# Row-wise infinity norm of an 8192 x 8192 float32 matrix: another split of the rows over partitions, the last quarter of them in smaller pieces, and the result stored in three parts

## The chip, the cores and the metric

The kernel runs on one core of one Trainium2 chip. The time is device microseconds of one execution, and a lower time is better. The core has a vector engine (DVE in the profile), which does all the arithmetic here, a sync engine (SP) and a scalar engine (ACT) whose queues issue transfers, and 16 DMA engines that carry the transfers between HBM and the on-chip memory SBUF. SBUF has 128 partitions, and the vector engine works on all of them side by side, each with its own stretch of data.

## The reference

For every row of the matrix the largest absolute value is wanted.

```python
def setup_inputs():
    rows = 8192
    cols = 8192
    return {
        "x": np.random.randn(rows, cols).astype(np.float32),
    }

def reference(x):
    return np.linalg.norm(x, ord=np.inf, axis=1)
```

The input has 8192 x 8192 x 4 bytes = 268.4 MB, and each element is read once. The output has 8192 numbers, 32 KB.

## The kernel before

The 8192 rows are 64 for each of the 128 partitions, and the kernel takes them two at a time (B = 2), so that there are 32 tiles. One tile `t` holds, in each partition, two adjacent rows, which are 16384 elements or 64 KB; over all partitions it has 8.39 MB. Two loops run over the tiles: the outer one over A = 8 blocks of 1024 rows, the inner one over N = 4 tiles in a block. Within a block each partition owns 8 adjacent rows (4 tiles of 2), so the addresses that neighbouring partitions read at the same time lie 8 rows of 32 KB apart, which is 256 KB.

For each tile, line 70 issues one load on the queue of the sync engine, and line 71 reduces it on the vector engine: one instruction reads 128 x 2 x 8192 elements and writes two numbers in each partition, the largest absolute values of the two rows, into `r_all`. The branch with `split` is never taken, since `split` is False. After the loops, line 78 stores `r_all` in one transfer, whose pieces in HBM are 8 numbers (32 bytes) long.

The pool `sbuf` has three buffers for `t`. The order on each engine is the order of the program. A load can be issued once the buffer that it goes into has been read by the reduce of three tiles earlier; the queue therefore holds up to three loads. Each load and store also takes one of eight completion semaphores (DMAHW0 to DMAHW7) in turn, and a transfer that gets a semaphore again waits, on the engine that issues it, until the transfer that had it before has landed.

Of the kernel before, what the change touches and what calls it, by code (L numbers as in the profile page):

```python
# [1 line left out]
logging.getLogger("concourse").setLevel(logging.ERROR)  # L3

# [1 line left out]

# [4 lines left out]


@with_exitstack
def kernel(
    ctx: ExitStack,
    tc: tile.TileContext,
    x: bass.AP,
    out: bass.AP,
    A: int = 8,
    B: int = 2,  # L20
    K: int = 4,
    BUFS: int = 3,
):
    nc = tc.nc
    P = nc.NUM_PARTITIONS

    rows, cols = x.shape
    assert rows % P == 0
    n_tiles = rows // P

    assert n_tiles % (A * B) == 0
    N = n_tiles // (A * B)
    x_t = x.rearrange("(a p n b) c -> a n p (b c)", p=P, a=A, n=N, b=B)
    out_t = out.rearrange("(a p n b) -> p a n b", p=P, a=A, n=N, b=B)

    bc = cols * B
    c_k = bc // K

    sbuf = ctx.enter_context(tc.tile_pool(name="sbuf", bufs=BUFS))
    outp = ctx.enter_context(tc.tile_pool(name="outp", bufs=1))  # L40

    r_part = outp.tile([P, N, K], mybir.dt.float32)
    r_all = outp.tile([P, A, N, B], mybir.dt.float32)

    for a in range(A):
        split = False
        for n in range(N):
            t = sbuf.tile([P, bc], x.dtype)
            t_b = t.rearrange("p (b c) -> p b c", b=B, c=cols)
            src = x_t[a, n]  # L50
            if split:
                for k in range(K):
                    nc.sync.dma_start(
                        out=t[:, k * c_k : (k + 1) * c_k],
                        in_=src[:, k * c_k : (k + 1) * c_k],
                    )
                    nc.vector.reduce_max(
                        out=r_part[:, n, k : k + 1],
                        in_=t[:, k * c_k : (k + 1) * c_k],
                        axis=mybir.AxisListType.X,  # L60
                        apply_absolute_value=True,
                    )
                nc.vector.reduce_max(
                    out=r_all[:, a, n, :],
                    in_=t_b[:],
                    axis=mybir.AxisListType.X,
                    apply_absolute_value=True,
                )
            else:
                nc.sync.dma_start(out=t[:], in_=src)  # L70
                nc.vector.reduce_max(  # L71
                    out=r_all[:, a, n, :],
                    in_=t_b[:],
                    axis=mybir.AxisListType.X,
                    apply_absolute_value=True,
                )

    nc.sync.dma_start(out=out_t[:], in_=r_all[:])


# [1 line left out]
_INS = ['x']  # L82
_OUTS = [((8192,), 'float32')]


# [23 lines left out]
```

## Time and profile before

| | before |
|---|---|
| median of 10 runs | 644.94 us (644.73 to 645.41) |
| the profiled execution | 644.73 us, span 642.7 us from the first to the last instruction |
| vector engine busy | 551.0 us, 86% of the span, 32 instructions |
| loads | 32, in 4096 packets of 64 KB (one for each partition and tile) |
| result's store | 1, 32 KB in 1024 packets of 32 bytes |
| bytes read from HBM | 268.44 MB, 418 GB/s over the span |

The span runs from the first instruction to the last; the time has about 2 us more, which lie around it. In the views of the profile, "SPq" is the queue of the sync engine, and "A <- B" in a wait reads "A waited for B". "DMA share" is the mean busy share of the 16 DMA engines, so 1.00 means that all of them were moving data all the time. The count of packets on the page, 5648, is the 4096 packets of the loads, the 1024 of the store, and 16 short completion packets for each of the 33 transfers (528). The figures in GB/s by slices of the span jump between 392 and 457, a step of 65 GB/s: in a slice of 16.07 us that is one packet of 64 KB more or less on each of the 16 engines.

### The profile page before, as it was taken

The numbers are of one execution on the slowest core, as the hardware profiler recorded it, in microseconds if no ns is written. First come the engines' busy times: TensorE is split into PE (matmuls) and PEld (weight loads), VectorE is DVE, ScalarE is ACT, GpSimd is POOL, SyncE is SP. The second block draws the span as 40 slices with busy tenths as digits, with TensorE's granted clock in tenths as the row PEclk, the third lists the DMA queues.
The fourth block names the chain that finished last, engine by engine and source line by source line (L and its number), as shares of the span: only waits on it lengthen the run. The fifth ranks groups of instructions, "written<-read, shape, count | busy, mean of one in ns | idle before, by whom it ended". The sixth has DMA issues, their size and how long they took to land.

```text
span 642.7 us, 139 instructions
## 1 busy us (share of the span) xinstructions
DVE 551.0 (86%) x32; POOL 0.2 (0%) x4
## 2 busy tenths in 40 slices
DVE  0588898888998888998888998888988888988888
POOL 0000000000000000000000000000000000000000
DMA  9999999999999999999999999999999999999960
GB/s 392 457 412 436 457 392 457 441 408 457 441 408 457 436 412 457 424 424 457 392 457 453 396 457 441 408 457 436 412 457 420 428 457 392 457 453 396 457 261 2
DMA packets 5648, 268.47 MB, mean 418 GB/s; under 512 B 1552, under 2 KB 1552, under 8 KB 1552
## 3 DMA queue, kind: packets, MB, share of 16 engines
q1 hardware_dynamic: 5648, 268.47, 96.6%
HBM read 268.44 MB, written 0.03 MB: 418 GB/s over the span
## 4 chain that ended last, share of the span: by engine, by line
DMA 70%; DVE 29%; issue 0%; SPq 0%
DMA t<-in_x_dram 70%; DVE r_all L71 29%; SPq L70 0%
## 5 line engine op out<-in xcount | busy, mean ns | idle before, releaser
L71 DVE TENSOR_REDUCE r_all<-t 128x2 f32<-128x16384 f32 x32 | 551.0, 17220 | 88.7 <-DMA t<-in_x_dram 88.7
L93 POOL MEMSET const-bfloat16-1.0<- 128x1 bf16 x1 | 0.1, 101 | 0.0
L93 POOL MEMSET const-uint8-127<- 128x1 uint8 x1 | 0.1, 101 | 0.0
L93 POOL MEMSET const-float32-0.0<- 128x1 f32 x1 | 0.1, 98 | 0.2 <-issue 0.2
L93 POOL MEMSET const-float32-1.0<- 128x1 f32 x1 | 0.1, 98 | 0.0
## 6 DMA issues: line engine op xcount, KB each, us to landing
t<-in_x_dram SPq DMA_DIRECT2D x32, 40.8
out_dram<-r_all SPq DMA_DIRECT2D x1, 32.0 KB, 2.2
```

The source lines that it names most:

```text
L71: nc.vector.reduce_max(out=r_all[:, a, n, :], in_=t_b[:], axis=mybir.AxisListType.X, apply_absolute_value=True,)
L93: nc = _bacc.Bacc("TRN2", target_bir_lowering=False, num_devices=1)
```

## The change

The rows are cut into two parts.

- **The bulk** is the first three quarters, 6144 rows, 48 for each partition. It is read in 24 tiles of two rows, each by one load of 64 KB per partition and one reduce, as before. There is one block (A = 1) in place of eight, so that each partition owns 48 adjacent rows (G = 24 tiles of B = 2), and neighbouring partitions read at addresses 1.5 MB apart. The 48 results of a partition lie in `r_bulk`, and one store issued on the queue of the scalar engine writes them (line 73), in pieces of 192 bytes.
- **The tail** is the last quarter, 2048 rows, 16 for each partition, which lie 512 KB apart from partition to partition. It goes through the same three buffers, two rows to a tile, but each row is loaded and reduced on its own, in the pieces that the table `TAIL` gives: eight rows whole (8192 elements, 32 KB per partition), five in halves, two in quarters, and the last one in pieces of 2048, 2048, 2048, 1024, 512 and 512 elements (8 KB down to 2 KB per partition). That is 32 loads and 32 reduces, where there were 8 and 8.
- **The partial results** of the tail's first 15 rows go into `part`, four places to a row, cleared by a memset at the start; one small reduce over `part` gives these rows' results in `r_tail`, and the scalar engine's queue stores them (line 88). The last row's first five pieces leave their results in the tile itself, in the spare columns just behind the row, so that the reduce of the last piece reads 512 elements and these five together and writes the row's final result to `r_fin`. The sync engine's queue stores that (line 99): one number for each partition.

```diff
+TAIL = (
+    [[8192]] * 8
+    + [[4096, 4096]] * 5
+    + [[2048] * 4] * 2
+    + [[2048, 2048, 2048, 1024, 512, 512]]
+)
...
-    A: int = 8,
+    G: int = 24,
     B: int = 2,
-    K: int = 4,
     BUFS: int = 3,
...
-    x_t = x.rearrange("(a p n b) c -> a n p (b c)", p=P, a=A, n=N, b=B)
-    out_t = out.rearrange("(a p n b) -> p a n b", p=P, a=A, n=N, b=B)
...
+    n_tail = len(TAIL)
+    assert n_tail % B == 0
+    n_bulk_rows = rows // P - n_tail
+    assert n_bulk_rows % (G * B) == 0
+    A = n_bulk_rows // (G * B)
+    split = n_bulk_rows * P
+    x_b = x[:split].rearrange("(a p n b) c -> a n p (b c)", p=P, a=A, n=G, b=B)
+    out_b = out[:split].rearrange("(a p n b) -> p a (n b)", p=P, a=A, n=G, b=B)
+    x_t = x[split:].rearrange("(p t b) c -> t p (b c)", p=P, b=B)
+    out_t = out[split:].rearrange("(p t) -> p t", p=P)
...
+    part = outp.tile([P, n_tail - 1, k_max], F32)
+    nc.vector.memset(part[:], 0.0)
+
+    def absmax(o, i):
+        nc.vector.reduce_max(out=o, in_=i, axis=X, apply_absolute_value=True)
 
     for a in range(A):
...
+        for n in range(G):
+            t = sbuf.tile([P, B * cols + 16], F32, tag="t")
+            nc.sync.dma_start(out=t[:, : B * cols], in_=x_b[a, n])
+            absmax(
+                r_bulk[:, a, n * B : (n + 1) * B],
+                t[:, : B * cols].rearrange("p (b c) -> p b c", b=B),
+            )
+    nc.scalar.dma_start(out=out_b, in_=r_bulk[:])
+
+    for i in range(0, n_tail, B):
+        t = sbuf.tile([P, B * cols + 16], F32, tag="t")
+        for j in range(B):
+            r = i + j
+            at = j * cols
+            last = r == n_tail - 1
+            for k, w in enumerate(TAIL[r]):
+                nc.sync.dma_start(
+                    out=t[:, at : at + w], in_=x_t[i // B][:, at : at + w]
+                )
+                if last and k == k_last - 1:
+
+                    absmax(r_tail[:, : n_tail - 1], part[:])
+                    nc.scalar.dma_start(
+                        out=out_t[:, : n_tail - 1], in_=r_tail[:, : n_tail - 1]
                     )
...
+                    absmax(r_fin[:], t[:, at : B * cols + k_last - 1])
+                elif last:
+                    absmax(
+                        t[:, B * cols + k : B * cols + k + 1], t[:, at : at + w]
                     )
...
+                else:
+                    absmax(part[:, r, k : k + 1], t[:, at : at + w])
+                at += w
+    nc.sync.dma_start(out=out_t[:, n_tail - 1 :], in_=r_fin[:])
```

On the sync engine's queue the end of the program stood like this before: seven of the 32 loads of whole tiles, the last one `t_156`, then the store.

```order
L70 DMA t_138<-in_x_dram 128x16384 [waits DMAHW6_49,DVE_49]
L70 DMA t_141<-in_x_dram 128x16384 [waits DMAHW7_49,DVE_49]
L70 DMA t_144<-in_x_dram 128x16384 [waits DMAHW0_49,DVE_49]
L70 DMA t_147<-in_x_dram 128x16384 [waits DMAHW1_49,DVE_49]
L70 DMA t_150<-in_x_dram 128x16384 [waits DMAHW2_49,DVE_49]
L70 DMA t_153<-in_x_dram 128x16384 [waits DMAHW3_49,DVE_49]
L70 DMA t_156<-in_x_dram 128x16384 [waits DMAHW4_49,DVE_49]
L78 DMA out_0_dram<-r_all_62 128x8x8 [waits DVE_49]
```

On the same queue the end is now this; `t_190` is the last tile, with the tail's rows 14 and 15.

```order
L82 DMA t_190<-in_x_dram 128x2048 [waits DMAHW7_49,DVE_49]
L82 DMA t_190<-in_x_dram 128x2048 [waits DMAHW0_49]
L82 DMA t_190<-in_x_dram 128x2048 [waits DMAHW1_49]
L82 DMA t_190<-in_x_dram 128x2048 [waits DMAHW2_49]
L82 DMA t_190<-in_x_dram 128x2048 [waits DMAHW3_49]
L82 DMA t_190<-in_x_dram 128x2048 [waits DMAHW4_49]
L82 DMA t_190<-in_x_dram 128x2048 [waits DMAHW6_49]
L82 DMA t_190<-in_x_dram 128x1024 [waits DMAHW7_49]
L82 DMA t_190<-in_x_dram 128x512 [waits DMAHW0_49]
L82 DMA t_190<-in_x_dram 128x512 [waits DMAHW1_49]
L99 DMA out_0_dram<-r_fin_63 128x1 [waits DMAHW2_49,DVE_49]
```

The last tile's one load has become ten. Only the first of them waits for the buffer (DVE); every one waits for the landing of the transfer that had its semaphore before, eight transfers earlier. DMAHW5 is skipped here, since the store of `r_tail` on the scalar engine's queue takes it. The store at the end waits for the final reduce alone and for a landing long past.

On the vector engine the last instructions are now these; before, there was one reduce of 128 x 16384 elements for each tile and nothing else.

```order
L63 TENSOR_REDUCE part_64<-t_190 128x1 [waits DMAHW2_49]
L63 TENSOR_REDUCE r_tail_62<-part_64 128x15 [waits DVE_49]
L63 TENSOR_REDUCE t_190<-t_190 128x1 [waits DMAHW3_49]
L63 TENSOR_REDUCE t_190<-t_190 128x1 [waits DMAHW4_49]
L63 TENSOR_REDUCE t_190<-t_190 128x1 [waits DMAHW6_49]
L63 TENSOR_REDUCE t_190<-t_190 128x1 [waits DMAHW7_49]
L63 TENSOR_REDUCE t_190<-t_190 128x1 [waits DMAHW0_49]
L63 TENSOR_REDUCE r_fin_63<-t_190 128x1 [waits DMAHW1_49,DVE_49]
```

Each reduce now waits for its own piece. The reduce that fills `r_tail` stands ahead of the last row's six, though the source has it behind five of them, and its store can go out while the last row is still on its way.

More of the change, by code (lines that the diff above doesn't have):

```diff
@@ L10 @@
 from concourse._compat import with_exitstack
+F32 = mybir.dt.float32
+X = mybir.AxisListType.X
+TAIL = (
[4 more added lines that the diff above has]
+)
 @with_exitstack
@@ L27 @@
     rows, cols = x.shape
[L28 to L32, printed above, removed]
-    x_t = x.rearrange("(a p n b) c -> a n p (b c)", p=P, a=A, n=N, b=B)
-    out_t = out.rearrange("(a p n b) -> p a n b", p=P, a=A, n=N, b=B)
-    bc = cols * B
-    c_k = bc // K
+    n_tail = len(TAIL)
[4 more added lines that the diff above has]
+    split = n_bulk_rows * P
@@ L39 @@
+    x_b = x[:split].rearrange("(a p n b) c -> a n p (b c)", p=P, a=A, n=G, b=B)
+    out_b = out[:split].rearrange("(a p n b) -> p a (n b)", p=P, a=A, n=G, b=B)
+    x_t = x[split:].rearrange("(p t b) c -> t p (b c)", p=P, b=B)
+    out_t = out[split:].rearrange("(p t) -> p t", p=P)
     sbuf = ctx.enter_context(tc.tile_pool(name="sbuf", bufs=BUFS))
     outp = ctx.enter_context(tc.tile_pool(name="outp", bufs=1))
-    r_part = outp.tile([P, N, K], mybir.dt.float32)
-    r_all = outp.tile([P, A, N, B], mybir.dt.float32)
@@ L45 @@
-    for a in range(A):
[L46 to L55, printed above, removed]
-                    )
[L57 to L61, printed above, removed]
-                    )
[L63 to L76, printed above, removed]
@@ L78 @@
-    nc.sync.dma_start(out=out_t[:], in_=r_all[:])
+    k_last = len(TAIL[-1])
+    r_bulk = outp.tile([P, A, G * B], F32)
+    r_tail = outp.tile([P, n_tail], F32)
+    r_fin = outp.tile([P, 1], F32)
+    k_max = max(len(r) for r in TAIL[:-1])
+    part = outp.tile([P, n_tail - 1, k_max], F32)
+    nc.vector.memset(part[:], 0.0)
+    def absmax(o, i):
+        nc.vector.reduce_max(out=o, in_=i, axis=X, apply_absolute_value=True)
+    for a in range(A):
+        for n in range(G):
[5 more added lines that the diff above has]
+            )
```

## The prediction

> **What bounds the kernel now.** I read the chain of work that ended last, then the windows by stage, then the groups and the waits. The chain of the page says that transfers and reduces share the end of the program, and its pieces in order of time show how:
>
> ```profile
> DMA 70%; DVE 29%; issue 0%; SPq 0%
> ...
> 0.73 0.38 SPq L70
> 1.11 0.06 issue
> 1.17 40.73 DMA t<-in_x_dram
> 41.90 0.02 issue
> 41.93 17.23 DVE r_all L71
> 59.16 0.02 issue
> 59.17 40.81 DMA t<-in_x_dram
> ...
> 581.67 40.77 DMA t<-in_x_dram
> 622.44 0.02 issue
> 622.46 17.22 DVE r_all L71
> ```
>
> The 29% look like a loop of load and reduce, in which a shorter reduce would help everywhere. They are not. A load takes 40.8 us from issue to landing, which is more than two tiles' time, since it stands behind two others in the queue. The windows (length, DVE busy, POOL busy, clock, DMA share, GB/s) say what is full:
>
> ```profile
> 0.00:22.00 22.00, 0.00 (x0) 0.20 (x4) 1.00 0.98 417
> 22.00:100.00 78.00, 68.88 (x4) 0.00 (x0) 1.00 1.00 434
> 100.00:200.00 100.00, 89.35 (x6) 0.00 (x0) 1.00 0.99 430
> ...
> 600.00:620.00 20.00, 17.87 (x2) 0.00 (x0) 1.00 1.00 433
> 620.00:622.40 2.40, 0.34 (x1) 0.00 (x0) 1.00 0.00 0
> 622.40:639.70 17.30, 17.22 (x1) 0.00 (x0) 1.00 0.00 0
> 639.70:642.67 2.97, 0.00 (x0) 0.00 (x0) 1.00 0.16 11
> ```
>
> From the start to 620 us the DMA engines have no idle time (0.98 to 1.00), so the loads bound this stretch and the reduces lie beside them. Behind it come three pieces in which no load moves: 2.4 us until the last landing is known, 17.22 us of the last reduce, and about 3 us for the store. The group and the timeline agree:
>
> ```profile
> L71 DVE TENSOR_REDUCE r_all<-t 128x2 f32<-128x16384 f32 x32 | 551.0, 17220 | 88.7 <-DMA t<-in_x_dram 88.7
> ...
> 22.61 17.22 DVE L71 TENSOR_REDUCE r_all<-t 128x2 f32<-128x16384 f32 x1 [22.61 <-DMA t<-in_x_dram]
> ...
> 603.12 17.22 DVE L71 TENSOR_REDUCE r_all<-t 128x2 f32<-128x16384 f32 x1 [2.13 <-DMA t<-in_x_dram]
> 622.46 17.22 DVE L71 TENSOR_REDUCE r_all<-t 128x2 f32<-128x16384 f32 x1 [2.13 <-DMA t<-in_x_dram]
> 639.71 0.40 SPq L78 DMA_DIRECT2D out_dram<-r_all  x1
> ```
>
> A tile takes 17.22 + 2.13 = 19.35 us, of which the vector engine idles 2.13. So 8.39 MB move in 19.35 us (433.5 GB/s), and 32 of them in 619.2 us. Call T the last landing, now at 622.44. The sum of the program is T, plus what the vector engine has left to do behind T, plus the store and the end.
>
> **The change part by part.**
>
> *The bulk, if its rate holds.* 24 loads and 24 reduces have the size and the waits of before, so they take 24 x 19.35 = 464.4 us as before. What is new is only where the addresses lie: 1.5 MB from partition to partition in place of 256 KB. No row shows another pitch. A gain is bounded, as the DMA share is already 1.00. A loss is bounded by no row but the slowest inner slice of the page, 392 GB/s, and its jumps are the counting of whole packets (65 GB/s is one on each engine):
>
> ```profile
> GB/s 392 457 412 436 457 392 457 441 408 457 441 408 457 436 412 457 424 424 457 392 457 453 396 457 441 408 457 436 412 457 420 428 457 392 457 453 396 457 261 2
> ```
>
> I take zero, since the rate did not move between windows (430 to 434) while the addresses ran through all blocks; the loss is the first rival below.
>
> *The tail's loads.* 8 loads become 32 with the same bytes. A load of 128 partitions is 128 packets, so 24 loads more are 3072 packets, 192 for each DMA engine. The price of a packet apart from its bytes isn't shown for these sizes; the only small packets are the store's, 1024 of 32 bytes and 16 of completion (5648 less 4096 of loads and 32 x 16 of their completions):
>
> ```profile
> DMA packets 5648, 268.47 MB, mean 418 GB/s; under 512 B 1552, under 2 KB 1552, under 8 KB 1552
> ```
>
> In the last window the engines are busy 0.16 x 2.97 us x 16 = 7.6 us for these 1040, 7.3 ns each. 192 x 7.3 ns = 1.40 us. The completion packets of the 24 loads, one on each engine, cost 24 x 7.3 ns = 0.18 us, and the two stores on the scalar engine's queue, which now lie beside loads, 2 x 9 packets on each engine, 0.13 us. Sum **+1.7 us** on T. From below the bound is 0 (the engines are full, so smaller packets can't move the bytes faster). From above it is the whole of the old store, which must fit 65 packets on each engine into its time to landing:
>
> ```profile
> t<-in_x_dram SPq DMA_DIRECT2D x32, 40.8
> out_dram<-r_all SPq DMA_DIRECT2D x1, 32.0 KB, 2.2
> ```
>
> 2.2 us / 65 = 34 ns, most of which is latency; 234 packets on each engine at that price are 8.0 us. I take 1.7, as the busy share is the nearer row.
>
> Here a rule speaks against small pieces. The first load of the chain, issued at 0.73, landed near 22.6, some 2.5 us later than the 19.35 us of its bytes; the following ones don't show it, as the cadence is 19.35 with three loads queued. The Trainium skill, SBUF — State Buffer, The DMA setup-cost knee, says that every transfer pays about 2 us that don't scale with its bytes, and advises the largest single transfer. Paid one after the other by 24 more loads, that is an estimate of 48 us more, and the sum would be near 680; the trace bears it out for the first load only.
>
> *The waits of these loads.* The issue of a load costs the sync engine 0.33 us and of the old store 0.40, less than the 0.6 us in which even the 2 KB piece moves:
>
> ```profile
> L70 SPq DMA_DIRECT2D t<-in_x_dram x32: 327/328/424, 0.7 to 581.7; - x32
> ...
> L78 SPq DMA_DIRECT2D out_dram<-r_all x1: 398/398/398, 639.7 to 639.7; - x1
> ```
>
> Each load also waits for the landing eight transfers earlier, with all later loads queued behind it on SP. A quarter of a row (1.05 MB) moves in 19.35/8 = 2.42 us. When the 1024-element piece may go out, the first quarter of row 14 has landed, and three of row 14 and three of row 15 are still ahead in the queue: 14.5 us of cover against 2.5 us of latency and 0.3 of issue. So the queue doesn't run dry, and the cost is nothing.
>
> *The end on the vector engine.* The 17.22 us behind T go. What comes in their place depends on the fixed cost f of a reduce, which no row shows by itself, since all 32 have one size. The bounds: f = 0 gives 17.22/16384 = 1.051 ns an element; an upper one is 0.3 us, three times the nearest short instruction, and that I take itself, **f = 0.10 us**:
>
> ```profile
> L93 POOL MEMSET const-bfloat16-1.0<- 128x1 bf16 x1 | 0.1, 101 | 0.0
> ```
>
> Then an element costs 17.12/16384 = 1.045 ns, and a reduce of 2048 takes 2.24, of 1024 1.17, of 512 0.635, of 517 (the final one) 0.64, and of the 60 of `part` 0.16 us. The last row's third quarter lands at T-2.42, the 1024 at T-1.21, the first 512 at T-0.60. The quarters ahead of them take less (2.24) than they need to land (2.42), and the small reduce into `r_tail` has 0.16 us there. So the third quarter runs from T-2.39 to T-0.15, the 1024 to T+1.04, the first 512 to T+1.70, and the final one to **T+2.36**, with 0.02 us for each start. With f = 0 it ends at T+1.9, with f = 0.3 at T+3.1. The saving is 17.22 - 2.36 = **14.86 us**, and what is late next is the same vector engine, by 2.4 us, then the store.
>
> *The memset* of 128 x 60 stands in the 22.61 us in which the vector engine has no data yet; without that cover it would cost some 0.1 us. *The store of* `r_bulk` goes out with a fifth of the program to run and that of `r_tail` while the last row loads, both on ACT, which has nothing else; uncovered, each would be a store at the end, 2.2 us.
>
> *The last store* has 8 packets on an engine where there were 64. The most that can save is 56 x 7.3 ns = 0.4 us; the other bound is +0.5, for short writes of 4 bytes. I take **-0.2**.
>
> *The sum*, on the profiled execution's own 644.73 (span 642.7): 644.73 + 1.7 - 14.86 - 0.2 = 631.4. That execution lies 0.2 below the median of the runs, 644.94, so I say **631.6 us**, 2.1% less.
>
> **The rivals.**
>
> *A. The new addresses slow the loads.* The partitions' streams that are read at one time lie multiples of 1.5 MB apart in the bulk and of 512 KB in the tail, in place of 256 KB. If such streams fall on the same part of HBM, all 619 us stretch. Against it: no loss at 256 KB, itself a power of two, with shares of 1.00. For it: nothing in the trace shows headroom, and 433 GB/s is all that was asked. It decides from 13.3/619.2 = 2.1%, a rate under 424 GB/s; the far end, 392 GB/s everywhere, gives 268.44 MB / 392 = 685 us of loads and 697 in all. Half-way between 433.5 and 392, 413 GB/s, it is 650 us of loads, 31 more: **662 us, slower** than before. A smaller loss, 0.4 to 2.1%, gives 634 to 644.
>
> The Trainium skill, DMA: Bandwidth & Descriptors, Latency and other measured facts, has a table for this under HBM row pitch at large powers of two: copies within HBM ran at 207 GB/s with a pitch of 512 KB against 214 at full rate, and lost more and more from 2 MB up. An estimate by that page, with 1.5 MB taken as 512 KB is, is 3.4% more transfer time, 21 us, and 652 in all; by it too the change would lose.
>
> *B. Small pieces cost more than I took.* At 34 ns a packet T is 8.0 us later in place of 1.7: **638 us**. The same range holds a vector engine that falls behind: from f = 0.27 us a quarter takes longer than its landing, and at 0.5 us eleven quarters add 2.5 us, and the last four reduces about 1 more, 635. Against both: busy packets of 7.3 ns.
>
> *C. The change doesn't overlap as it says.* If the wait for eight landings empties the queue, each of the 11 quarters and 3 shorter loads pays up to 2.5 us anew: 14 x 2.5 = 35 us, 666. It needs a cover under 2.8 us where I count 14.5.
>
> **How the numbers follow.** Forecast (629 to 634): 0.57. Rival B (634 to 639): 0.13. A with a small loss (634 to 644): 0.10. A past its deciding point: 0.14. C: 0.03. Below 629, by a rate that rises beyond 433.5 or free packets and a short end together: 0.03. The range is 629 to 643: it takes in the forecast, B and nearly all of A's small losses, and leaves out 0.20. A difference of 0.2%, 1.3 us, is about what a measurement of this kernel can tell from no change. Faster is 0.57 + 0.13 + 0.09 + 0.03 = 0.82; the same (643.6 to 646.2) 0.03, from A's cases about its point; slower 0.12 + 0.03 = 0.15.
>
> **What would show it.** In the profile of the changed kernel: idle gaps of about 2.13 us ahead of the 24 bulk reduces and a DMA share of 1.00 (the rate holds; longer gaps with share 1.00 are rival A, gaps with a lower share in the tail are C); a last landing near 624; a row for a reduce of 512 elements, which gives f; some 2.4 us from the last landing to the end of the last reduce; and the store as before. I would be wrong above all if the bulk's cadence isn't 19.35 us.

## The result, and the profile after

The changed kernel takes **630.39 us** (median of 8 runs, 630.24 to 630.50) against 644.89 us (29 runs, 644.72 to 645.46). The ratio is 0.9774, with a 95% interval of 0.9765 to 0.9782: 2.3% less time. The forecast was 631.6 in a range of 629 to 643. The profiled execution has 630.26 us and a span of 628.5.

The chain of the page, which before read 70% transfers and 29% reduces, now has more of the reduces:

```profile
DMA 65%; DVE 32%; issue 1%; another core or an unknown queue 0%; SPq 0%
```

That says nothing of the bound, as it said nothing before: load and reduce hand over to each other all the way, and the chain may follow either. The windows tell what is full. Here are those of the changed kernel (length, DVE busy, POOL busy, clock, DMA share, GB/s): the bulk, the tail, and the last microseconds of the loads.

```profile
22.00:467.00 445.00, 396.05 (x23) 0.00 (x0) 1.00 1.00 434
460.00:622.00 162.00, 158.21 (x32) 0.00 (x0) 1.00 1.00 426
...
622.00:623.00 1.00, 1.00 (x1) 0.00 (x0) 1.00 0.91 348
623.00:624.00 1.00, 1.00 (x2) 0.00 (x0) 1.00 0.12 43
```

The bulk moves at 434 GB/s, as the loads did before (433 to 434 from 22 us on). The tail has the same full share of 1.00 and 426 GB/s: the engines are as busy, with a little less to show for it. The loads now go on to 623 or so. The timeline shows the beginning, the end of the bulk, and what the vector engine does behind the last loads:

```profile
23.25 17.22 DVE L63 TENSOR_REDUCE r_bulk<-t 128x2 f32<-128x16384 f32 x1 [22.33 <-DMA t<-in_x_dram]
...
467.94 17.22 DVE L63 TENSOR_REDUCE r_bulk<-t 128x2 f32<-128x16384 f32 x1 [2.14 <-DMA t<-in_x_dram]
...
616.62 0.34 ACTq L88 DMA_DIRECT2D out_dram<-r_tail  x1
621.39 4.01 DVE L63 TENSOR_REDUCE t<-t 128x1 f32<-128x2048 f32 x3 [0.20 <-DMA t<-in_x_dram]
625.43 0.69 DVE L63 TENSOR_REDUCE r_fin<-t 128x1 f32<-128x517 f32 x1
626.15 0.35 SPq L99 DMA_DIRECT2D out_dram<-r_fin  x1
```

The first reduce starts at 23.25 (before 22.61), and the 24th at 467.94. At the end the third quarter of the last row has waited 0.20 us for its landing; from there on the vector engine has no gap until 626.12. The store of `r_tail` went out at 616.62, beside the last row's loads. The last load, by the sync engine's line 82, and the last store, by line 99, from issue to landing:

```profile
L82 SPq DMA_DIRECT2D t<-in_x_dram x1: 328/328/328, 611.6 to 611.6; - x1
...
DMA to landing us min/median/max: 12.3/12.3/12.3
```

```profile
L99 SPq DMA_DIRECT2D out_dram<-r_fin x1: 347/347/347, 626.1 to 626.1; - x1
...
DMA to landing us min/median/max: 1.4/1.4/1.4
```

So the last landing T is 611.6 + 12.3 = 623.9, and the vector engine ends 2.2 us behind it, where it ended 17.2 behind. Last, the groups of reduces by shape (mean ns behind the comma), which give the fixed cost that the trace of before couldn't show:

```profile
L63 DVE TENSOR_REDUCE part<-t 128x1 f32<-128x8192 f32 x8 | 68.9, 8678 | 0.3 <-DMA t<-in_x_dram 0.3
L63 DVE TENSOR_REDUCE part<-t 128x1 f32<-128x4096 f32 x10 | 43.6, 4414 | 0.9 <-DMA t<-in_x_dram 0.9
...
L63 DVE TENSOR_REDUCE t<-t 128x1 f32<-128x2048 f32 x3 | 6.8, 2282 | 0.3 <-DMA t<-in_x_dram 0.2
L63 DVE TENSOR_REDUCE t<-t 128x1 f32<-128x1024 f32 x1 | 1.2, 1207 | 0.0
...
L63 DVE TENSOR_REDUCE t<-t 128x1 f32<-128x512 f32 x1 | 0.7, 676 | 0.0
```

From 512 to 8192 elements it is 8002 ns for 7680 elements, 1.042 ns each, and 676 - 512 x 1.042 = 143 ns are left as the fixed cost. The Trainium skill, VectorE: DVE Perf Modes, Side-by-side: where the cycles go, puts some 150 cycles of start and 8 of pipe fill at 0.96 GHz on an instruction, an estimate of 165 ns; the trace is somewhat below it. Reduces that follow one another without a gap overlap a little: by their means the last three ahead of the final one (2.28, 1.21 and 0.68 us) add up to 4.17 us, and in the timeline they last 4.01, so that each begins some 0.08 us before the one ahead of it has ended.

### The profile page after: what moved, and what is told of

Its sections match the earlier page's. It is cut to its first block, busy times and chain, and to the rows that moved or that the text cites. A ratio compares the mean times of both kernels' runs of the same rounds, so it can differ in the third digit from the quotient of the medians.

```text
span 628.5 us, 196 instructions
## 1 busy us (share of the span) xinstructions
DVE 552.7 (88%) x58; POOL 0.2 (0%) x4
## 4 chain that ended last, share of the span: by engine, by line
DMA 65%; DVE 32%; issue 1%; another core or an unknown queue 0%; SPq 0%
DMA t<-in_x_dram 65%; DVE r_bulk L63 23%; DVE part L63 8%; DVE t L63 1%; DVE r_fin L63 0%; SPq L68 0%; SPq L82 0%
## 5 line engine op out<-in xcount | busy, mean ns | idle before, releaser
L63 DVE TENSOR_REDUCE r_bulk<-t 128x2 f32<-128x16384 f32 x24 | 413.3, 17220 | 71.0 <-DMA t<-in_x_dram 71.0
L63 DVE TENSOR_REDUCE part<-t 128x1 f32<-128x4096 f32 (+2 forms) x26 | 130.0, 5067 | 1.3 <-DMA t<-in_x_dram 1.3
L63 DVE TENSOR_REDUCE t<-t 128x1 f32<-128x2048 f32 (+2 forms) x5 | 8.6, 1746 | 0.3 <-DMA t<-in_x_dram 0.2
```

Source lines behind the costliest of these rows:

```text
L63: nc.vector.reduce_max(out=o, in_=i, axis=X, apply_absolute_value=True)
```

## The experiments

Four questions: does the new pitch cost or gain anything, what is a packet's price, what sets the end behind the last landing, and what do the early stores bring.

### The pitch alone

**The bulk back at 256 KB**, with the tail of the change:

```diff
-    G: int = 24,
+    G: int = 4,
```

> The changed kernel with the bulk in six blocks of 8 rows per partition, so that the partitions' rows lie 256 KB apart as before; the tail is untouched. Theory 1 (the pitch is free at these values): 630.4 us, within 0.4, and a bulk cadence of 19.33 to 19.35 us. Theory 2 (the 1.5 MB pitch gave the bulk its slightly shorter cadence, 19.334 against 19.350): 0.4 us longer, 630.8. Theory 3 (the 1.5 MB pitch made the first load late, 23.25 against 22.61): the first reduce starts near 22.6 again, and the time is 0.6 us shorter, 629.8.

Measured: 630.18 us (5 runs, 629.80 to 630.43), ratio to before 0.9769 (0.9756 to 0.9782); the changed kernel's is 0.9774. The two can't be told apart by the time. The first reduce starts at 22.83, where the changed kernel has it at 23.25. Theory 1 holds for the time. Theory 2 is out: from the first reduce to the 24th the cadence is 19.342 us here, and 19.334 to 19.352 in six executions with 1.5 MB. Of theory 3 a late start of some tenths of a microsecond is left, as the starts listed below show, but the rest of an execution scatters by as much.

**The kernel before at 2 MB and at 512 KB**, whose other parts are unchanged but for the store, which has 128 packets of 256 bytes and 512 of 64:

```diff
-    A: int = 8,
+    A: int = 1,
```

That is 2 MB; A = 4 gives 512 KB.

> The kernel before with one block in place of eight: each partition owns 64 adjacent rows, 2 MB apart from partition to partition; loads, reduces and buffers as before. Theory 1 (loads into SBUF don't feel the pitch): the cadence stays 19.35 us, and the time is 644.9 less up to 0.6 for the store, which now has 128 packets of 256 bytes in place of 1024 of 32. Rival (large powers of two alias in HBM): the copies that the Trainium skill tells of lost 23% at 2 MB (164 against 214 GB/s), which here would be a cadence near 25 us and a time near 830 us.

> The kernel before with four blocks: 16 adjacent rows per partition, 512 KB apart, the pitch of the changed kernel's tail. Theory 1: cadence 19.35 us, time 644.9 less up to 0.4 for a store of 512 packets of 64 bytes. Rival (aliasing): 3.4% more transfer time, 21 us, time near 666 us.

Measured: 644.90 us at 512 KB (10 runs, ratio 0.9998, 0.9989 to 1.0007), and 652.38 us at 2 MB (4 runs, 649.78 to 653.34, ratio 1.0108, 1.0089 to 1.0126). So 512 KB costs nothing that the time shows. In its one profiled execution the first reduce starts at 22.97 in place of 22.61 and the last one at 622.99 in place of 622.46, and the shorter store gives most of that half microsecond back. At 2 MB neither side's number came: it is a loss, but of 1.1% and not 29%. The timeline of the 2 MB kernel says where it is:

```profile
25.95 17.22 DVE L71 TENSOR_REDUCE r_all<-t 128x2 f32<-128x16384 f32 x1 [25.95 <-DMA t<-in_x_dram]
47.30 17.22 DVE L71 TENSOR_REDUCE r_all<-t 128x2 f32<-128x16384 f32 x1 [4.13 <-DMA t<-in_x_dram]
68.95 17.22 DVE L71 TENSOR_REDUCE r_all<-t 128x2 f32<-128x16384 f32 x1 [4.43 <-DMA t<-in_x_dram]
89.21 17.22 DVE L71 TENSOR_REDUCE r_all<-t 128x2 f32<-128x16384 f32 x1 [3.05 <-DMA t<-in_x_dram]
108.54 17.22 DVE L71 TENSOR_REDUCE r_all<-t 128x2 f32<-128x16384 f32 x1 [2.11 <-DMA t<-in_x_dram]
...
631.78 17.22 DVE L71 TENSOR_REDUCE r_all<-t 128x2 f32<-128x16384 f32 x1 [2.12 <-DMA t<-in_x_dram]
```

The first landing is 3.3 us late and the next three 2.0, 2.3 and 0.9; from the fifth on the idle time is 2.11 to 2.4 us, nearly the 2.13 of before. By the windows the loads run at 393 GB/s up to 90 us and at 434 afterwards, with addresses 2 MB apart all the time. The share is 0.98 even in the slow part, so the engines weren't waiting; each packet took longer:

```profile
0.00:90.00 90.00, 52.45 (x4) 0.20 (x4) 1.00 0.98 393
90.00:620.00 530.00, 471.70 (x28) 0.00 (x0) 1.00 1.00 434
```

What changes in the first 90 us? The last packets of the program give a hint. Windows of half a microsecond count the whole of a packet where it starts (a share of 0.30 for each 64 KB), so they show when the 16 engines begin their last one. In the kernel before it is 618.5 to 620:

```profile
618.00:618.50 0.50, 0.50 (x1) 0.00 (x0) 1.00 0.00 0
618.50:619.00 0.50, 0.50 (x1) 0.00 (x0) 1.00 2.12 918
619.00:619.50 0.50, 0.50 (x1) 0.00 (x0) 1.00 1.82 786
619.50:620.00 0.50, 0.50 (x1) 0.00 (x0) 1.00 0.91 393
620.00:620.50 0.50, 0.34 (x1) 0.00 (x0) 1.00 0.00 0
```

In the 2 MB kernel the shares from 625.5 to 629 add up to 15 packets, and the last packet of the sixteenth engine is one of those that start between 624.5 and 625. So they are spread over some 4 us, more than twice as wide:

```profile
624.50:625.00 0.50, 0.50 (x1) 0.00 (x0) 1.00 2.42 1049
625.00:625.50 0.50, 0.50 (x1) 0.00 (x0) 1.00 0.00 0
625.50:626.00 0.50, 0.50 (x1) 0.00 (x0) 1.00 0.30 131
626.00:626.50 0.50, 0.50 (x1) 0.00 (x0) 1.00 1.21 524
626.50:627.00 0.50, 0.50 (x1) 0.00 (x0) 1.00 1.21 524
627.00:627.50 0.50, 0.50 (x1) 0.00 (x0) 1.00 1.51 655
...
628.50:629.00 0.50, 0.50 (x1) 0.00 (x0) 1.00 0.31 131
```

That led to a new theory: the 16 engines' streams, which start in step, hinder each other at a large pitch, each loses a different amount, and once they have drifted apart the hindrance is gone, as long as the queue never runs empty. Its rival is a cost paid once, at the first touches of the memory.

**One buffer, at 256 KB and at 2 MB**, so that every load starts from idle engines:

```diff
-    BUFS: int = 3,
+    BUFS: int = 1,
```

> The kernel before (256 KB pitch) with one buffer, so that each load starts when the engines are idle and nothing is queued behind it. A tile is 21.9 us of load, 17.22 of reduce and some 0.05 between them, so 32 of them take 1253 us, and with the end about 1258 us.

> The same with a pitch of 2 MB. In e2 the first landing came 3.3 us late and the next three 2.0, 2.3 and 0.9, then the cadence was 19.35 again while the landings of one load on the 16 engines had drifted apart. Theory 1 (16 streams that start in step collide, and queued loads drift apart until they don't): every load that starts from idle engines is late by about 3.3 us, 32 x 3.3 = 106 us more than with one buffer at 256 KB, about 1364 us. Rival (something that is paid once, at the first touches of the memory): only the first loads are late, up to 9 us more, about 1267 us.

Measured: 1258.58 and 1359.69 us (one run each), 101 us apart. The waits of the two, first 256 KB, then 2 MB:

```profile
DVE r_all L71 <- DMA t<-in_x_dram: 702.5, 32, 22.7
```

```profile
DVE r_all L71 <- DMA t<-in_x_dram: 804.3, 32, 26.2
```

(804.3 - 702.5)/32 = 3.2 us: with 2 MB every load that starts from idle engines is late, not the first alone, by as much as the first load with three buffers was (3.3). A cost of the first touches is out.

The records of single packets and landings in the same traces bear out the drift. With three buffers at 2 MB a packet of 64 KB took 2.81, 2.64, 2.58 and 2.51 us on the average of the first four loads and 2.42 to 2.45 from the fifth on (before, 2.48 in the first load and 2.42 to 2.43 in all others). From the first to the last of the 16 engines' landings it is 1.7, 1.8, 3.3 and 4.2 us in those four loads and 4.2 to 4.8 in all later ones, against 0.7 before: the engines drift apart while the packets are slow, and stay apart when the packets are quick. With one buffer at 2 MB the landings lie 1.0 to 2.9 us apart and the packets never become quick, 2.75 us on the average against 2.49 at 256 KB. Drift and speed go together in all of this; that the first is the cause of the second is the likeliest reading and no more. Which part of the memory the streams share isn't shown, nor whether it matters that 2 MB is a power of two and 1.5 MB isn't: no other large pitch was run.

### A packet's price

The kernel before with a gap of 16 bytes behind every 512 elements in SBUF, and a reduce that skips the gaps:

```diff
-            t = sbuf.tile([P, bc], x.dtype)
+            t = sbuf.tile([P, B, cols // 512, 516], x.dtype)
...
-                nc.sync.dma_start(out=t[:], in_=src)
+                nc.sync.dma_start(
+                    out=t[:, :, :, :512],
+                    in_=src.rearrange("p (b k c) -> p b k c", b=B, c=512),
+                )
```

> The kernel before with each tile cut in SBUF into 32 stretches of 512 elements per partition with a gap of 16 bytes between them, so that a load of the same bytes is 4096 packets of 2 KB in place of 128 of 64 KB; as many loads and reduces as before. 31 more packets for each partition and tile are 32 x 8 x 31 = 7936 more on each DMA engine. Theory 1 (7.3 ns a packet, the prediction's term): 7936 x 7.3 ns = 58 us more, about 703 us, cadence 21.2 us. Rival B (34 ns): 270 us more, about 915 us. Packets that cost nothing: 645 us.

Measured: 714.77 us (one run). The page counts 132624 packets, and by the timeline, which stands behind it, the reduces start some 21.5 us apart:

```profile
DMA packets 132624, 268.47 MB, mean 377 GB/s; under 512 B 1552, under 2 KB 1552, under 8 KB 132624
```

```profile
671.05 17.22 DVE L55 TENSOR_REDUCE r_all<-t 128x2 f32<-128x16384 f32 x1 [4.31 <-DMA t<-in_x_dram]
692.53 17.22 DVE L55 TENSOR_REDUCE r_all<-t 128x2 f32<-128x16384 f32 x1 [4.26 <-DMA t<-in_x_dram]
```

69.9 us more for 7936 packets on each engine is 8.8 ns a packet. The prediction's 7.3 was near, rival B's 34 is out.

### What sets the end

**Whole rows in the tail:**

```diff
-TAIL = (
-    [[8192]] * 8
-    + [[4096, 4096]] * 5
-    + [[2048] * 4] * 2
-    + [[2048, 2048, 2048, 1024, 512, 512]]
-)
+TAIL = [[8192]] * 16
```

> The changed kernel with every row of the tail loaded and reduced whole (16 loads of 32 KB per partition, in place of 32 loads down to 2 KB). Theory 1 (a packet costs about 9 ns apart from its bytes; the end is what the vector engine has left to do behind the last landing): 128 packets fewer on each DMA engine bring the last landing forward by 1.1 us, and 8.68 us of reduce stand behind it in place of 2.24: 630.4 - 1.1 + 6.4 = 635.7 us. Rival B of the prediction (small pieces are dear, 34 ns a packet): the last landing comes 4.4 us earlier and the time is 632.4 us.

Measured: 636.72 us (4 runs, 636.46 to 637.49), ratio 0.9873 (0.986 to 0.9887). The last row's reduce:

```profile
623.40 8.69 DVE L58 TENSOR_REDUCE r_fin<-t 128x1 f32<-128x8192 f32 x1 [0.76 <-DMA t<-in_x_dram]
632.11 0.35 SPq L94 DMA_DIRECT2D out_dram<-r_fin  x1
```

It waited for its landing at 623.38 and ends 8.7 us behind it. So 6.3 of the change's 14.5 us come from the pieces smaller than a row, and 8.2 from all the rest: the tail loaded and reduced row by row, and the other layout and order of the stores. Rival B, by which T would have come 4.4 us earlier, is out here too. The expectation was 1 us low: T came forward by 0.5 us where 128 packets at 9 ns gave 1.1, and the rest lies behind the last reduce (2.65 us from 632.11 to the span's end, in the changed kernel 2.33 from 626.15).

**Three pieces of 1024 in the last row:**

```diff
-    + [[2048, 2048, 2048, 1024, 512, 512]]
+    + [[2048, 2048, 1024, 1024, 1024, 512, 512]]
```

> The changed kernel with the last row in pieces of 2048, 2048, 1024, 1024, 1024, 512, 512 in place of 2048, 2048, 2048, 1024, 512, 512. A reduce of 1024 takes 1.21 us and needs 1.21 to land, so the last of the three 1024 should end at T, where the 2048 and 1024 of the changed kernel end 1.05 behind T. Theory (the end is the vector engine's backlog behind the last landing): the last reduce ends at T+1.4 in place of T+2.2, 0.8 us off, 629.6 us. Rival (the landings, not the backlog, set the end): no change, 630.4 us.

Measured: 630.34 us (5 runs, 630.07 to 631.56), no difference that can be told from the changed kernel. The profiled execution is one of the longer ones (631.11): T is 615.0 + 9.9 = 624.9 and the last reduce ends at 626.91, T+2.0 in place of T+1.4. In its timeline the six reduces ahead of the last one have no gap:

```profile
617.53 8.65 DVE L63 TENSOR_REDUCE t<-t 128x1 f32<-128x2048 f32 x6
...
626.22 0.69 DVE L63 TENSOR_REDUCE r_fin<-t 128x1 f32<-128x518 f32 x1
```

The arithmetic of the expectation was wrong: when a piece of 2048 has just landed, the next one of 1024 lands 1.2 us later, but the 2048 takes 2.28 to reduce. This halving puts the vector engine about 1 us behind, and pieces of 1024, whose reduces start 1.13 us apart and which land 1.2 to 1.35 apart, make good only 0.1 to 0.2 us each. The backlog starts one piece earlier, and is hardly smaller.

**A slow taper**, with the sizes chosen by that arithmetic, **and the same with the bulk at 256 KB**:

```diff
-    [[8192]] * 8
-    + [[4096, 4096]] * 5
-    + [[2048] * 4] * 2
-    + [[2048, 2048, 2048, 1024, 512, 512]]
+    [[8192]] * 7
+    + [[640, 7552], [4992, 3200], [2432, 5760], [4352, 3840], [4480, 3712]]
+    + [[2432, 3328, 2432], [3072, 2816, 2304], [2432, 2176, 1664, 1920]]
+    + [[1792, 1792, 1664, 1536, 1408]]
```

> The changed kernel with another table: seven rows whole, then 640 and 7552, five rows in halves and thirds of slowly falling size, and the last rows in 2432, 2176, 1664, 1920 and 1792, 1792, 1664, 1536, 1408 elements. A reduce of w elements takes 0.145 us + 1.0417 ns x w, a landing 0.07 us + 1.1733 ns x w, so each piece may be only about a tenth smaller than the one before if the vector engine isn't to fall behind; halving, as in the changed kernel and in e8, leaves it 1.05 us behind. Theory: the last reduce ends 1.7 us behind the last landing in place of 2.2, and one load less on the way: 0.5 to 0.8 us off, 629.6 to 629.9 us. Rival (this end is not set by the backlog): no change against the changed kernel in the same call.

> The same table, and the bulk with 256 KB from partition to partition as in e1. Theory (a first load of 16 streams in step is late by 0.4 us at 1.5 MB): 0.2 to 0.4 us less than e11, 629.4 us, with the first reduce starting at 22.6 to 22.9 us. Rival (the pitch is nothing here): the same as e11.

**And the changed kernel once more in the same series:**

> The changed kernel once more, beside the other three on the same chip: 630.4 us, and a first reduce that starts near 23.2 us, if the late start belongs to the pitch and not to one execution.

Measured: 630.29 us (629.95 to 630.87) with the slow taper, 630.11 (629.97 to 631.17) with 256 KB besides, and 630.88 (630.73 to 630.92) for the changed kernel. The slow taper's end, with its last load issued at 610.6 and landing 14.1 us later:

```profile
617.22 7.58 DVE L63 TENSOR_REDUCE t<-t 128x1 f32<-128x1792 f32 x4
617.34 0.34 ACTq L88 DMA_DIRECT2D out_dram<-r_tail  x1
624.84 1.62 DVE L63 TENSOR_REDUCE r_fin<-t 128x1 f32<-128x1412 f32 x1
```

The last reduce ends at 626.46, 1.8 us behind T = 624.7; with 256 KB at 625.86, 1.8 behind 624.1; in the changed kernel once more at 626.78, 2.3 behind 612.2 + 12.3 = 624.5. So the backlog did shrink by the half microsecond that was expected. The times point the same way, by 0.6 and 0.8 us in this series, but their runs overlap, the ratios to before (0.9774 for both, 0.9782 for the changed kernel) have intervals that overlap, and the changed kernel's own medians in two series differ by 0.5. Whether these tables beat it stays open; if so, by about 0.1%.

The starts of the first reduce, read off each profile: with 1.5 MB 23.25, 23.09, 23.01, 22.95, 22.92 and 22.89, mean 23.02; with 256 KB 22.61, 22.83, 22.74 and 22.71, mean 22.72. The larger pitch makes the first load 0.3 us later on the average.

### The stores

The stores of the bulk and of the tail are put behind the last reduce on the sync engine's queue, with the last row's result copied beside the other 15:

```diff
-    nc.scalar.dma_start(out=out_b, in_=r_bulk[:])
...
-    nc.sync.dma_start(out=out_t[:, n_tail - 1 :], in_=r_fin[:])
+    nc.vector.tensor_copy(out=r_tail[:, n_tail - 1 :], in_=r_fin[:])
+    nc.sync.dma_start(out=out_b, in_=r_bulk[:])
+    nc.sync.dma_start(out=out_t, in_=r_tail[:])
```

> The changed kernel with the stores of the bulk and of the tail's results issued one after the other on the sync engine's queue behind the last reduce (the last row's result is first copied beside the other 15), in place of three stores of which two go out early. Theory 1 (the early stores save one issue and little else, since stores at the end overlap): one more issue of 0.35 us and a copy of about 0.15 us, 630.9 us. Rival (each store at the end pays its own landing): 1.4 to 2 us more, 632 us.

Measured: 630.69 us (4 runs, 630.26 to 631.77), beside 630.88 for the changed kernel in the same series. But the edit did less than it was meant to. The bulk's store, last but one in the source, waits for nothing but results that are long there, and goes out when the last load has been issued:

```profile
611.52 0.35 SPq L96 DMA_DIRECT2D out_dram<-r_bulk  x1
...
626.03 0.15 DVE L95 COPY r_tail<-r_fin 128x1 f32<-128x1 f32 x1
626.22 0.34 SPq L97 DMA_DIRECT2D out_dram<-r_tail  x1
```

So only the store of `r_tail` has been moved to the end, joined with the last row's. That costs a copy of 0.15 us and nothing that the time shows, so storing `r_tail` early brought nothing either. A bulk store at the very end of this kernel wasn't run. The 2 MB kernel comes near it: it stores all 8192 results at its end, in 128 packets, and that store lands 1.5 us behind its issue, 0.1 us later than the changed kernel's last one. What shortened the end is thus the small number of packets, 128 in place of 1024, much more than the early start.

## Why the prediction was right

By its own steps, on the profiled executions (644.73 and 630.26, 14.5 us apart):

- **The bound.** Right: the DMA share is 1.00 through bulk and tail, and the loads set T. One reading was wrong, though no term rested on it. The prediction took the window from 620 to 622.4 us, with a share of 0.00, for 2.4 us in which no load moves. The window counts a packet where it starts, and a packet of 64 KB takes 19.35/8 = 2.42 us; the engines were working on their last ones. With pieces of 2 KB at the end the share goes on to 623, and the landing is at 623.9.
- **The bulk's rate.** Right within 0.3 us: the 24th reduce starts at 467.94, 22.61 + 23 x 19.35 = 467.66 before. The first load is 0.64 later in this execution (0.3 in the mean), and the cadence, (467.94 - 23.25)/23 = 19.334, gives some of it back. But there was luck in the zero. The reason given for it, that the rate didn't move while the addresses ran through all blocks, says nothing of another pitch, since the pitch was 256 KB all the way; the kernel with 2 MB lost 7.5 us, and no row of before could tell that 1.5 MB would not.
- **The tail's loads, +1.7.** From the 24th landing to T it is 623.9 - 467.9 = 156.0 us, against 8 x 19.35 = 154.8: +1.2. With the start, T is 1.4 later. A packet of 2 KB measured 8.8 ns in place of 7.3; the tail, with 234 more on each engine, should then show 2.1 us. In the second profiled execution of the changed kernel it does, nearly: from 467.8 to 624.5 it is 156.7, +1.9. The 1.7 lies between the two, and T scatters by half a microsecond between executions.
- **The waits of the loads.** Right: in the tail the vector engine waits 1.5 us in all for pieces, and the share stays at 1.00. Rival C didn't occur, nor did the set-up cost paid in series, which would have shown in every one of the 32 loads.
- **The end on the vector engine, T+2.36.** Measured T+2.2; the mechanism is right, and part of the nearness is luck. The fixed cost f is 0.143 us and not 0.10, an element 1.042 and not 1.045 ns, within the bounds; four reduces at that f would have ended some 0.15 us later. The overlap of 0.08 us between neighbours, which the prediction didn't have, takes that back, and the last quarter of the last row, in its three small pieces, took 2.5 us to land and not 2.42.
- **The last store, -0.2.** Mis-sized: it lands 1.4 us behind its issue, not 2.2, and from the last reduce to the span's end it is 0.6 us less. The price of 7.3 ns, the busy share of the old store, was too low for how long a store takes to land. The stores of the same 32 KB in 1024, 512 and 128 packets (kernel before, 512 KB, 2 MB) landed after 2.2, 1.8 and 1.5 us, which is 12 to 13 ns for each packet on an engine; the 56 fewer here give 0.7. The other bound, +0.5 for pieces of 4 bytes, had no row behind it, and nothing of the kind shows.
- **Around the span** the time has 1.8 us in place of 2.0, which the sum didn't foresee; why isn't known.

So the sum missed by 1.1 us: 0.3 in T, 0.1 on the vector engine, 0.4 at the store and 0.3 around the span. All four lie on the same side, so none of them has hidden another.

- **Rival A** was rightly a rival, and wrongly sized. The pitch matters, but with a full queue only for the first loads: 0.3 us once at 1.5 MB, 3.3 us and some more in the next three loads at 2 MB, and hardly anything later while the queue stays full. The Trainium skill's rule (DMA: Bandwidth & Descriptors, Latency and other measured facts), that copies within HBM lose 3% at 512 KB and 23% at 2 MB, shows here as no loss at 512 KB and 1.1% at 2 MB; with an emptied queue it is 3.2 us in some 22, 15%, for every load, which is the nearest that these runs come to it.
- **Rival B** fell by the 8.8 ns of a packet and by the kernel with whole rows. Its deciding f of 0.27 us was reckoned with 1.051 ns an element; by the prediction's own formula, in which an element gets cheaper as f grows, it is about 0.3, and the measured 0.143 is below either.

## What to carry to other kernels

Where transfers are the bound, as here, the work that the vector engine did beside them cost nothing, and what it did behind the last landing cost all of it: make the last pieces small, and write the result in few packets. The pieces should shrink only as fast as the engine's margin over the transfers allows, since every halving left it about one of the smaller pieces behind. Going from 64 KB down to 2 KB brought 15 of 17 us here; a finer choice of sizes took another half microsecond off the backlog, which the times can't tell from nothing. Small pieces were cheap as long as the queue was full: some 9 ns a packet and no set-up time that shows.

## What the hardware showed that was not expected

A pitch of 2 MB hindered the loads only until the 16 engines had drifted apart: they ran at 393 GB/s for 90 us and then at 434 for the rest, with the same pitch, while their landings of one load went from 1.7 us apart to over 4 and stayed there. With one buffer, where the engines come to rest between tiles, each load paid 3.2 us. Bandwidth measured on transfers that each start from rest may thus be lower than that of a stream that never stops.
